# First FFN of a hybrid decoder layer on one Trainium2 core: its RMSNorm from a token-major copy of x, the embedding stores on another queue, and the first 18 steps from a written list

## The chip, the cores and the metric

The kernel runs on 1 core of one Trainium2 chip. The metric is device microseconds of one execution: the median of 3 runs of the kernel before is 1090.26 us (1090.19 to 1090.28). The profile is of one further execution, which took 1090.34 us and whose profiled span is 1088.6 us.

## What is computed

One layer for 512 tokens of width 1024: a SwiGLU FFN, a mixing sub-layer (spatial gating beside a state-space scan), a second FFN, a gated per-layer embedding and a final norm. The change lies in the first FFN and in the embedding's projection, which the kernel computes at its very start.

```python
def rmsnorm(x, g):
    y = x * lax.rsqrt(jnp.mean(x * x, axis=-1, keepdims=True) + EPS)
    return y * g
def swiglu(x, w_gate, w_up, w_down):
    return (jax.nn.silu(x @ w_gate) * (x @ w_up)) @ w_down

h = h + 0.5 * swiglu(rmsnorm(h, ffn1_norm), ffn1_w_gate, ffn1_w_up, ffn1_w_down)
...
h = h + gate * (p @ ple_w_proj)
```

All matrices are float32. Each product is made of three passes of TensorE in a rounded float32 type: high part times high part, high times low, low times high. So every weight and every activation is first split: ScalarE casts the high part (`hi`), VectorE subtracts it from the original (`lo`).

## The kernel before

**Layout.** Activations lie feature-major: `h[0]` to `h[7]` are 128 features by 512 tokens each. FFN weights come in blocks of 128 x 1024 float32 (512 KB): `raw` and `rawb` are the buffers in which they land, `whi`/`wlo` their two parts.

**The FFN in groups of 256 hidden features.** Eleven groups. Group 0 is computed plainly, in four steps (gate and up, upper and lower half of the input features, 128x512 matmuls). Groups 1 to 10 use Strassen's scheme: seven products of 128x256 matmuls (L624) of sums of weight blocks with sums of activation blocks. The sums of activations (`xfa`, `xfb`: the forms x, T1, T2, T3, T4) are made once, by `Early` (L499 to L568): `Early.x` scales h by the norm's gain, `Early.form` adds the blocks (L564, L566), `Early.t` splits the sum (L549, L551), `Early.t1` forms T1 in the buffer `embt` (L535) and lets GpSimd subtract its low part (L539). The sums of weights are made by DMAs of GpSimd's queue that add a second block to one that has landed (L639, L642, L676), and one by VectorE (L634).

**The norm.** The FFN's matmuls run on h times the gain, without the factor 1/rms of a token; that factor comes in behind them, at the gate (L728) and later. `Norm.add` squares h[d] on ScalarE (L247, L250) and adds it up on GpSimd (L251, seven adds); `Norm.sums` lets TensorE add over the features (L261, `ones`, one column for each of 4 token chunks); `of_sums` works out 1/sqrt in 11 small VectorE instructions on 128x4 (L217 to L222); `diagonals` makes two 128x512 tiles of it (L281 to L285); `spread` multiplies them with ones on TensorE (L298), `kept` copies that to SBUF (`rall`, L304).

**Steps and their order.** A `Step` has a load, a split, a product (TensorE) and an `after`. `run` (L347) walks over all steps: product i, split of step i+2, `after` of step i-1, loads six steps ahead. What it records is the order of each engine's queue: TensorE, ScalarE, VectorE and SP run exactly in that order. Steps 0 and 1 are the embedding's two projections, 2 to 5 the plain group, 6 to 14 Strassen group 1 with two down-projection steps in it, and from 15 on group 2. `also` hangs further work on a step (L946 to L959): for instance the squares and T3 on the split of steps 3 and 4, T2 on that of step 6, T1 on 7, T4 on 9.

**The embedding's result** (8 tiles of 128x512, 2 MB) is stored to DRAM by five DMAs of GpSimd's queue (L870), and read back at the kernel's end. Its source tiles are `embt` (two tiles), `p7`, `u2` and two `rawd`, buffers which the FFN uses again later: `embt` for T1.

Of the kernel before, what the change touches and what calls it, by code (L numbers as in the profile page):

```python
# [16 lines left out]

# [20 lines left out]
G_PARTS = (1, 2, 2, 2, 2, 2)  # L38
# [7 lines left out]
LOADS, MIX_LOADS = 6, 4  # L46

# [36 lines left out]
def layer_kernel(ctx: ExitStack, tc: tile.TileContext, a: dict, out: bass.AP):  # L84
# [242 lines left out]

    class Step:


        def __init__(self, product, load=None, sums=None, split=None, after=(), urgent=False):
            self.product, self.load, self.sums, self.split = product, load, sums, split

            self.after, self.urgent = after, urgent
# [11 lines left out]
    def run(steps, opened):  # L346


        n = len(steps)
        held = []  # L350

        def do(i, what):
            if 0 <= i < n and getattr(steps[i], what):
                getattr(steps[i], what)()

        loaded = 0
        for i in range(-3, n + 2):
# [7 lines left out]
            if i in opened:  # L365
                open_region("right", opened[i])
                while held:
                    do(held.pop(0), "load")
            late = 0 <= i - 1 < n and not steps[i - 1].urgent
            do(i + 2, "cast")  # L370
            if 0 <= i - 2 < n and len(steps[i - 2].after) > 1:
                steps[i - 2].after[1]()
            for what in ("split", "after") if late else ("after", "split"):
                if what == "split":
                    do(i + 2, "split")
                    do(i + 3, "sums")
                elif 0 <= i - 1 < n and steps[i - 1].after:
                    steps[i - 1].after[0]()
            do(i - 1, "post")
            do(i, "rest")  # L380

    def also(step, what, fn):

        if what == "after":
            old = step.after[0] if step.after else lambda: None
            step.after = (lambda: (old(), fn()),) + tuple(step.after[1:])
        else:
            old = getattr(step, what) or (lambda: None)
            setattr(step, what, lambda: (old(), fn()))
# [5 lines left out]
    class Parts:  # L395
# [18 lines left out]
        def split(self, raw=None, x=""):  # L414
# [5 lines left out]
            return self.hi, self.lo  # L420

# [81 lines left out]
    class Early:  # L503
# [8 lines left out]
        def x(both, lower):  # L512

            blocks = []
            for e in both:
                hg = e.hg[lower] = sb(("ghi", "glo")[lower], (P, 2, T))
                for k in range(2):
# [3 lines left out]
                    else:  # L521
                        nc.scalar.activation(hg[:, k], h[d], AF.Copy, scale=col(e.name, d))
                blocks.append((hg.rearrange("p k (s t) -> p s k t", s=2), (e.a, e.b)[lower][:, 0:2]))
            for t, to in blocks:
                nc.scalar.copy(to[:, :, 0], t)
            for t, to in blocks:
                nc.vector.tensor_tensor(to[:, :, 1], t, to[:, :, 0].bitcast(F32), ALU.subtract)

        @staticmethod
        def t1(both):  # L530

            f = sb("embt", (P, 2, 2, HT))
            for n, e in enumerate(both):
                x11, x12 = (e.hg[0].rearrange("p k (s t) -> p s k t", s=2)[:, s] for s in range(2))
                nc.vector.tensor_tensor(f[:, n], x11, x12, ALU.subtract)  # L535
            for n, e in enumerate(both):
                nc.scalar.copy(e.a[:, 1, 0], f[:, n])
            for n, e in enumerate(both):
                nc.gpsimd.tensor_tensor(e.a[:, 1, 1], f[:, n], e.a[:, 1, 0].bitcast(F32), ALU.subtract)  # L539

        @staticmethod
        def t(both, i, formed=False):


            if not formed:
                Early.form(both, i)
            blocks = [(e.f[:, (3, 2, 4).index(i) % 2], e.b[:, {3: 2, 2: 3, 4: 4}[i]]) for e in both]
            for f, to in blocks:
                nc.scalar.copy(to[:, 0], f)  # L549
            for f, to in blocks:  # L550
                nc.vector.tensor_tensor(to[:, 1], f, to[:, 0].bitcast(F32), ALU.subtract)  # L551

        @staticmethod
        def form(both, i):
            n = (3, 2, 4).index(i) % 2
            for e in both:
# [8 lines left out]
                else:  # L565
                    nc.vector.scalar_tensor_tensor(  # L566
                        f, x11 if i == 2 else x21, -1.0, other, ALU.mult, ALU.subtract
                    )  # L568

# [25 lines left out]
    class Group:  # L595


        def __init__(self, src, xfs, shared, j):
            self.src, self.xfs, self.shared, self.j = src, xfs, shared, j
            self.last = j == sum(G_PARTS) - 1  # L600
# [28 lines left out]
        def steps(self):  # L629
# [6 lines left out]
            def load7():  # L636
# [11 lines left out]
                (lambda half=half: (self.gate_sum(half), self.gate(half)), lambda half=half: self.times_r(half))  # L648
                for half in range(2)
            ]  # L650
            if self.j == 1:
                gates[1] = (lambda: (self.gate_sum(1), self.gate(1), up()), gates[1][1])
# [15 lines left out]
        def step(self, i, w, raw, to, fresh, loads, sums, after):  # L668
# [3 lines left out]
            def split():  # L672
                parts[0] = w.split(self.s1 if raw else None)
                if i == 6:

# [14 lines left out]
        def plain_steps(self):  # L690


            def step(w, i, which, lower):
                w_parts = {}

                def split():
                    w_parts[0] = w.split()
# [16 lines left out]
                s = Step(product, lambda: self.load((w, i)), None, split, urgent=lower)  # L714
# [9 lines left out]
        def plain_gate(self):  # L724
            self.g = sb("g", (P, 2, 2, HT))
            for m, ps in enumerate(self.ps["gate"]):
                t = self.g[:, :, m]
                nc.vector.tensor_tensor(t, by_half(ps), by_half(self.shared["r"]), ALU.mult)  # L728
                nc.scalar.activation(t, t, AF.Silu)

        def plain_finish(self):
            for m, ps in enumerate(self.ps["up"]):
                t = self.g[:, :, m]
                nc.vector.tensor_tensor(t, t, by_half(self.shared["r"]), ALU.mult)
# [1063 lines left out]
```

## Time and profile before

| what | value |
|---|---|
| median of 3 runs | 1090.26 us |
| the profiled execution | 1090.34 us |
| its span | 1088.6 us |
| TensorE matmuls busy | 1073.7 us (99%) |
| VectorE busy | 783.3 us (72%) |
| ScalarE busy | 515.3 us (47%) |
| GpSimd busy | 154.1 us (14%) |
| DMA | 161.67 MB, mean 149 GB/s |

Times in a timeline are microseconds from the span's start. A row gives start, duration, engine, line, operation, output<-inputs, sizes and count; in brackets stands the idle time of the engine before it and what ended that. TensorE's matmuls overlap in a pipeline: a row's duration is longer than the distance between two starts, so lost time is read from the starts.

### The profile page before, as it was taken

How to read it: one execution, taken by the hardware profiler on the slowest of the kernel's cores; microseconds unless marked ns; L12 is line 12 of the kernel's file. 1: busy time of each engine (PE TensorE's matmuls, PEld its weight loads, DVE VectorE, ACT ScalarE, POOL GpSimd, SP SyncE). 2: the span in 40 equal slices, each digit the busy share in tenths (PEclk: the TensorE clock that was granted, in tenths of full speed). 3: DMA queues.
4: the chain of work that ended last, by engine and by line, in shares of the span. 5: the costliest groups of instructions: out<-in, count | busy, mean ns of one | idle time of the engine just before them, and what ended most of it. 6: DMA issues, size and time to landing. Idle time of an engine off the chain costs nothing.

```text
span 1088.6 us, 16562 instructions
## 1 busy us (share of the span) xinstructions
PE 1073.7 (99%) x6687; PEld 949.8 (87%) x6687; DVE 783.3 (72%) x1078; ACT 515.3 (47%) x711; POOL 154.1 (14%) x139
## 2 busy tenths in 40 slices
PE   9989999999999999999999999999999999999997
PEld 7889999999998788787878888899999999999886
DVE  7797776666667596756897756678766776767766
ACT  6554443444444455474653434354444344344554
POOL 3400000000000300134133000000000000000311
PEclk9999999999999999999999999999999999999998
DMA  9758756675624233444342333567766666643412
GB/s 363 201 141 232 199 152 181 180 193 137 173 60 135 64 93 102 147 129 134 99 131 77 100 94 113 189 144 213 208 163 169 193 183 185 168 123 99 146 46 78
DMA packets 49037, 161.67 MB, mean 149 GB/s; under 512 B 5568, under 2 KB 5824, under 8 KB 48960
## 3 DMA queue, kind: packets, MB, share of 16 engines
q1 hardware_dynamic: 38288, 124.80, 34.2%
q0 software_dynamic: 9232, 33.56, 17.2%
q10 hardware_dynamic: 1440, 2.26, 0.7%
q8 instruction: 52, 0.85, 0.3%
q14 instruction: 25, 0.20, 0.1%
HBM read 156.33 MB, written 4.26 MB: 148 GB/s over the span
## 4 chain that ended last, share of the span: by engine, by line
PE 87%; DVE 7%; ACT 3%; issue 2%; DMA 1%; SPq 0%; POOL 0%; DVEq 0%; ACTq 0%; POOLq 0%
PE mm L624 18%; PE a L624 14%; PE sm L200 10%; PE sm L199 10%; PE sm L201 10%; PE mm L200 4%; PE mm L201 4%; PE mm L199 4%; PE a L199 3%; PE a L201 3%; PE a L200 3%; DVE wlo L428 2%; ACT whi L424 1%; DMA h<-in_x 1%; PE sm L261 1%
## 5 line engine op out<-in xcount | busy, mean ns | idle before, releaser
L424 ACT CAST whi<-raw 128x1024 fp32r<-128x1024 f32 x138 | 144.4, 1046 | 161.0 <-issue 56.8
L428 DVE TENSOR_TENSOR wlo<-raw,whi 128x1024 fp32r<-128x1024 f32 x137 | 172.8, 1261 | 61.9 <-ACT whi L424 60.8
L624 PE MATMUL mm<-xfb,whi 128*128 128x256 f32 x960 | 166.5, 276 | 0.1
L624 PEld LDWEIGHTS mm<-xfb,whi 128*128 128x128 f32 x960 | 145.9, 188 | 1.8 <-ACT a L738 0.2
L624 PE MATMUL mm<-xfb,wlo 128*128 128x256 f32 x480 | 133.1, 277 | 0.4 <-DVE wlo L428 0.3
L201 PE MATMUL sm<-ghi,wlox 128*128 128x512 f32 x296 | 116.3, 393 | 0.0
L200 PE MATMUL sm<-glo,whix 128*128 128x512 f32 x296 | 115.9, 392 | 0.0
L199 PE MATMUL sm<-ghi,whix 128*128 128x512 f32 x296 | 115.2, 389 | 0.0
L624 PE MATMUL a<-xfb,whi 128*128 128x256 f32 x640 | 111.2, 277 | 0.9 <-DVE g L756 0.9
L624 PEld LDWEIGHTS a<-xfb,whi 128*128 128x128 f32 x640 | 97.7, 188 | 3.1 <-issue 1.5
L624 PEld LDWEIGHTS mm<-xfb,wlo 128*128 128x128 f32 x480 | 90.2, 188 | 0.7 <-DVE wlo L428 0.7
L624 PE MATMUL a<-xfb,wlo 128*128 128x256 f32 x320 | 88.7, 277 | 1.1 <-DVE wlo L428 1.1
L428 DVE TENSOR_TENSOR wlox<-rawd,whix 128x1024 fp32r<-128x1024 f32 (+1 forms) x40 | 45.7, 1142 | 58.6 <-ACT whix L424 58.6
L428 DVE TENSOR_TENSOR wlo<-rawb,whi 128x1024 fp32r<-128x1024 f32 x52 | 64.7, 1246 | 25.1 <-ACT whi L424 24.9
L762 ACT ACTIVATE g<-g 128x512 f32<-128x512 f32 x40 | 25.3, 632 | 108.9 <-DVE g L761 108.9
L639 POOL DMA_DIRECT2D raw<-in_ffn_gu x20 | 17.2, 860 | 387.4 <-DVE h L816 122.9
L251 POOL TENSOR_TENSOR ssum<-ssum,tmp 128x512 f32<-128x512 f32 x33 | 50.2, 1522 | 123.7 <-ACT tmp L250 122.8
L816 DVE SCALAR_TENSOR_TENSOR h<-sm,h 128x512 f32<-128x512 f32 x96 | 63.2, 684 | 5.1 <-PE sm L201 4.5
L424 ACT CAST whi<-rawb 128x1024 fp32r<-128x1024 f32 x52 | 54.1, 1043 | 26.7 <-DVE rawb L634 20.0
L201 PEld LDWEIGHTS sm<-ghi,wlox 128*128 128x128 f32 x296 | 55.6, 188 | 11.7
L199 PEld LDWEIGHTS sm<-ghi,whix 128*128 128x128 f32 x296 | 55.7, 188 | 10.8 <-DVE h L816 0.2
L200 PEld LDWEIGHTS sm<-glo,whix 128*128 128x128 f32 x296 | 55.5, 188 | 10.8
(412 smaller groups left out, 2529.7 us busy)
## 6 DMA issues: line engine op xcount, KB each, us to landing
raw<-in_ffn_gu SPq DMA_DIRECT2D x56, 512.0 KB, 5.7
rawd<-in_ffn_down SPq DMA_DIRECT2D x40, 512.0 KB, 4.1
rawb<-in_ffn_gu SPq DMA_DIRECT2D x32, 512.0 KB, 5.1
raw<-in_ffn_gu POOLq DMA_DIRECT2D x30, 512.0 KB, 5.6
raw<-in_w_in SPq DMA_DIRECT2D x29, 512.0 KB, 3.7
s<-in_ffn_gu SPq DMA_DIRECT2D x20, 512.0 KB, 6.7
s<-in_ffn_gu POOLq DMA_DIRECT2D x20, 512.0 KB, 8.5
raw<-in_w_out SPq DMA_DIRECT2D x16, 512.0 KB, 3.6
```

The source lines that it names most:

```text
L199: nc.tensor.matmul(ps, whi, xhi, start=first, stop=False)
L200: nc.tensor.matmul(ps, whi, xlo, start=False, stop=False)
L201: nc.tensor.matmul(ps, wlo, xhi, start=False, stop=last)
L251: self.engines[i].tensor_tensor(self.totals[i], self.totals[i], sq, ALU.add)
L261: nc.tensor.matmul(ps[:, c : c + 1], part[:, c * P : (c + 1) * P], ones[:, 0:1], start=part is t, stop=part is not t or more is None,)
L424: nc.scalar.copy(self.hi[:, : self.n], self.raw[:, : self.n])
L428: nc.vector.tensor_tensor(self.lo[:, :n], self.raw[:, :n], self.hi[:, :n].bitcast(F32), ALU.subtract)
L624: nc.tensor.matmul(o, wt[:, c], xt, start=fresh and p == m == n == 0, stop=last and n == 2, skip_group_check=True,)
L639: nc.gpsimd.dma_start(w21.raw, self.src[0], accum_op=ALU.add)
L762: nc.scalar.activation(t, t, AF.Silu)
L816: nc.vector.scalar_tensor_tensor(h[d], ps[d], 0.5, h[d], ALU.mult, ALU.add)
```

## The change

Four things are changed together.

1. **The norm of the first FFN** is a `RowNorm`. A second copy of x, token-major (`x_rows`, four chunks of 128 tokens by 1024 features), is a further input. Four DMAs of 512 KB bring it into `whix`, `wlox`, `g` and `s1`, buffers that are idle at that time. Four ScalarE instructions square a chunk and give the sum of a row as accumulator output: the 128x4 sums are there without GpSimd's adds and without TensorE's `sums`.
2. **Where it is asked for**: SP issues the four loads behind the last weight load of the plain group and of product 1 and ahead of the other loads of group 1.
3. **The five stores** of the embedding's result go to SP's queue, behind the loads of group 1.
4. **The first 18 steps' order** is written out: `ENTRY` lists pieces of the tasks (`split3:1` is the first piece of the split of step 3), `run` takes them in that order and everything else as before. To that end the helpers became generators that `yield` between instructions. T2, T4 and T1 are hung on the splits of steps 4, 5 and 6.

```diff
+    class RowNorm(Norm):
+        def load(self, *chunks):
+            for c in chunks:
+                self.rows[c] = sb(self.tags[c], (P, D))
+                nc.sync.dma_start(self.rows[c], self.src[c])
+        def add(self, *chunks):
+            if 0 in chunks:
+                self.squares = sb("rtok", (P, NC))
+            for c in chunks:
+                t = self.rows[c]
+                nc.scalar.activation(t, t, AF.Square, accum_out=self.squares[:, c : c + 1])
+                yield
...
+        for entry in order.split():
+            name, _, count = entry.partition(":")
+            for _ in islice(tasks[name], int(count) if count else None):
+                pass
+        for task in tasks.values():
+            for _ in task:
+                pass
...
     def store_embedding():
         for to, t in stores:
-            nc.gpsimd.dma_start(to, t)
+            nc.sync.dma_start(to, t)
...
-        norm.behind(steps[at:], D, lambda r: (shared.update(r=r), groups[0].plain_gate()))
+        norm.behind([steps[i] for i in (2, 2, 3)] if at else steps, D, gates)
...
-    ffn1_norm = Norm()
+    ffn1_norm = RowNorm(a["x_rows"], "whix", "wlox", "g", "s1")
...
-    also(steps[3], "split", lambda: (squares(0, 1), Early.x(early, 1), squares(2, 3)))
-    also(steps[4], "split", lambda: (Early.t(early, 3), squares(4, 5, 6, 7), store_embedding()))
-    also(steps[6], "split", lambda: Early.t(early, 2))
...
+    also(steps[6], "load", lambda: ffn1_norm.load(0, 1, 2, 3))
+    also(steps[3], "split", lambda: Early.x(early, 1))
+    also(steps[9], "load", store_embedding)
+    also(steps[4], "split", lambda: Early.t(early, 3))
+    also(steps[4], "split", lambda: Early.t(early, 2))
+    also(steps[5], "split", lambda: ffn1_norm.add(0, 1, 2))
+    also(steps[6], "split", lambda: ffn1_norm.add(3))
+    also(steps[5], "split", lambda: Early.form(early, 4))
+    also(steps[6], "split", lambda: Early.t1(early))
+    also(steps[5], "split", lambda: Early.t(early, 4, True))
```

**SP's queue, from the loads of group 1 on.** `rawb_150` is the last weight of the plain group, `rawb_178` that of product 1, the rest is for the products behind it. Before:

```order
L408 DMA rawb_150<-in_ffn_gu 128x1024
L408 DMA rawb_178<-in_ffn_gu 128x1024
L408 DMA raw_212<-in_ffn_gu 128x1024
L641 DMA s_59_215<-in_ffn_gu 128x1024
L408 DMA raw_218<-in_ffn_gu 128x1024
L408 DMA rawb_280<-in_ffn_gu 128x1024
L408 DMA rawd_475<-in_ffn_down 128x512
```

Now:

```order
L475 DMA rawb_178<-in_ffn_gu 128x1024
L354 DMA whix_180<-in_x_rows 128x1024
L354 DMA wlox_182<-in_x_rows 128x1024
L354 DMA g_184<-in_x_rows 128x1024
L354 DMA s_55_186<-in_x_rows 128x1024
L475 DMA raw_226<-in_ffn_gu 128x1024
L726 DMA s_65_229<-in_ffn_gu 128x1024
L475 DMA raw_232<-in_ffn_gu 128x1024
L475 DMA rawb_285<-in_ffn_gu 128x1024
L967 DMA emb_dram<-embt_262 128x1024
L967 DMA emb_dram<-p_72_265 128x512
```

The four row loads stand ahead of four weight loads, and the stores, which were not on this queue, behind them.

**VectorE's queue, around the norm's small instructions.** The place is the one between the plain group's last two products. Before, behind the diagonals (the rows end with the gate of the plain group):

```order
L285 TENSOR_TENSOR tmp_457<-ident_72,tokp_452 128x512
L428 TENSOR_TENSOR wlo_462<-raw_212,whi_461 128x1024
L566 SCALAR_TENSOR_TENSOR ghi_318<-glo_264,ghi_318 128x512
L566 SCALAR_TENSOR_TENSOR glo_320<-glo_267,glo_320 128x512
L535 TENSOR_TENSOR embt_468<-ghi_168 128x512
L535 TENSOR_TENSOR embt_468<-ghi_171 128x512
L728 TENSOR_TENSOR g_505<-sm_282,rall_503 128x2x256
```

Now, the rows ahead of the norm's first small instructions (`nv`, `ny`):

```order
L650 SCALAR_TENSOR_TENSOR glo_275<-glo_223,glo_275 128x512
L614 TENSOR_TENSOR embt_370<-ghi_167 128x512
L634 TENSOR_TENSOR xfb_110<-ghi_272,xfb_110 128x512
L634 TENSOR_TENSOR xfb_112<-glo_275,xfb_112 128x512
L504 TENSOR_TENSOR wlo_401<-rawb_178,whi_400 128x1024
L614 TENSOR_TENSOR embt_370<-ghi_171 128x512
L233 TENSOR_SCALAR nv_435<-rtok_323 128x4
L234 TENSOR_SCALAR ny_436<-nv_435 128x4
```

T4's and T1's work stood behind the norm's small instructions and now stands ahead of them; the first write of `embt_370` has to wait until the store of `embt_262`, the same memory, has landed.

**GpSimd's queue.** Before:

```order
L251 TENSOR_TENSOR ssum_259<-ssum_259,tmp_277 128x512
L870 DMA emb_dram<-rawd_308 128x1024
L639 DMA raw_212<-in_ffn_gu 128x1024
L642 DMA s_59_215<-in_ffn_gu 128x1024
L251 TENSOR_TENSOR ssum_259<-ssum_259,tmp_326 128x512
L870 DMA emb_dram<-rawd_311 128x1024
L251 TENSOR_TENSOR ssum_259<-ssum_259,tmp_329 128x512
```

Now, the whole of it up to group 2:

```order
L724 DMA raw_226<-in_ffn_gu 128x1024
L727 DMA s_65_229<-in_ffn_gu 128x1024
L620 TENSOR_TENSOR xfa_109<-embt_370,xfa_109 128x512
L620 TENSOR_TENSOR xfa_111<-embt_370,xfa_111 128x512
L724 DMA raw_609<-in_ffn_gu 128x1024
```

Adds and stores are gone from it; the two accumulating loads and T1's two subtractions, which both were there before, follow each other. On TensorE the only difference is that the eight one-column matmuls of `sums` (L261) are gone.

## Prediction before the run

> **What bounds the kernel now.** First the busy times of the page, then TensorE's own timeline, then windows of it.
>
> ```profile
> PE 1073.7 (99%) x6687; PEld 949.8 (87%) x6687; DVE 783.3 (72%) x1078; ACT 515.3 (47%) x711; POOL 154.1 (14%) x139
> ```
>
> TensorE is busy 99% of the span, and the change takes from it eight one-column matmuls. So it can pay only where TensorE stands still or runs slowly in the first 18 steps, up to about 80 us. The distance between two starts shows these places: elsewhere it is 0.23 us for a 128x512 matmul (34.69 to 34.92 below) and 0.11 for a 128x256 one (53.98 to 54.09).
>
> ```profile
> 34.69 0.39 PE L200 MATMUL sm<-xfb,whi 128*128 128x512 f32 x1
> 34.92 0.40 PE L201 MATMUL sm<-xfb,wlo 128*128 128x512 f32 x1
> 36.41 1.05 PE L261 MATMUL sm<-ones,ssum 128*128 128x1 f32 x8 [1.09 <-POOL ssum L251]
> 37.33 0.48 PE L199 MATMUL mm<-xfb,whi 128*128 128x512 f32 x1
> ...
> 50.36 0.28 PE L624 MATMUL mm<-xfb,wlo 128*128 128x256 f32 x1
> 51.47 0.39 PE L624 MATMUL mm<-xfb,wlo 128*128 128x256 f32 x1 [0.28 <-DVE wlo L428]
> ...
> 53.98 0.28 PE L624 MATMUL mm<-xfb,wlo 128*128 128x256 f32 x1
> 54.09 0.47 PE L624 MATMUL a<-xfb,whi 128*128 128x256 f32 x2
> 55.31 0.38 PE L624 MATMUL a<-xfb,wlo 128*128 128x256 f32 x1 [0.75 <-DVE wlo L428]
> ...
> 60.71 0.28 PE L624 MATMUL mm<-xfb,wlo 128*128 128x256 f32 x1
> 62.00 0.50 PE L624 MATMUL a<-xfa,whi 128*128 128x256 f32 x2 [1.00 <-ACT u L746]
> 62.34 0.28 PE L624 MATMUL a<-xfa,wlo 128*128 128x256 f32 x1
> ...
> 67.50 0.40 PE L201 MATMUL sm<-ghi,wlo 128*128 128x512 f32 x1
> 68.80 0.48 PE L624 MATMUL a<-xfb,whi 128*128 128x256 f32 x2 [0.91 <-DVE g L756]
> ```
>
> The next view is TensorE's windows; the columns are length, busy time with count of PE, PEld, DVE, ACT and POOL, the granted clock, DMA share and GB/s.
>
> ```profile
> 35.18:38.59 3.41, 2.32 (x15) 1.95 (x15) 3.33 (x5) 1.65 (x3) 1.18 (x1) 1.00 0.34 126
> 38.59:42.01 3.42, 3.42 (x10) 2.66 (x9) 3.01 (x16) 2.00 (x3) 0.00 (x0) 0.50 0.84 251
> 59.07:62.49 3.42, 2.42 (x21) 2.21 (x20) 3.39 (x4) 2.08 (x4) 0.00 (x0) 1.00 0.39 77
> ```
>
> Three losses can be read:
> - **The sums.** From 34.92 to 37.33 are 2.41 us where one matmul takes 0.23: 2.18 lost, waiting for GpSimd's adds and in the eight one-column matmuls.
> - **The half clock.** The 3.42 us behind it ran at a granted clock of 0.50: 1.71 lost.
> - **Four waits for split operands**: 50.36 to 51.47 (1.11, of which three matmuls take 0.34: 0.77), 54.09 to 55.31 (1.22 less 0.23: 0.99), 60.71 to 62.00 (1.29 less 0.11: 1.18), 67.50 to 68.80 (1.30 less 0.23: 1.07). Together 4.01, and 0.11 at each restart (62.00 to 62.34 is 0.34 where two take 0.23), 0.44 in all: 4.45.
>
> The sum is 8.3 us. That is all there is to win, 0.8%.
>
> **The change part by part.**
>
> *The norm's sums.* Removed: eight squares on ScalarE, seven adds on GpSimd, eight matmuls. Added: four squares of 128x1024 with an accumulator.
>
> ```profile
> 30.07 0.63 ACT L250 ACTIVATE tmp<-h 128x512 f32<-128x512 f32 x1 [0.43 <-POOL ssum L251]
> 40.42 0.20 ACT L951 ACTIVATE warm<-ones 128x1 f32<-128x1 f32 x1
> ...
> L424 ACT CAST whi<-raw 128x1024 fp32r<-128x1024 f32 x138 | 144.4, 1046 | 161.0 <-issue 56.8
> ```
>
> Eight times 0.63 is 5.0 us. No row shows an accumulator output; a square of 128x1024 lies between the cast's 1.05 and, if the sum comes out by an instruction of its own, 1.05 + 0.20: 4.2 to 5.0 for four. I take 5.0, no difference; ScalarE's order puts the last square ahead of T1's casts, so it is done before VectorE reaches the norm. It costs nothing on TensorE. The 2.18 us of the first loss go.
>
> *VectorE without GpSimd beside it.*
>
> ```profile
> 24.16 2.05 DVE L428 TENSOR_TENSOR wlo<-raw,whi 128x1024 fp32r<-128x1024 f32 x1 [0.34 <-ACT whi L424]
> 31.67 3.57 DVE L428 TENSOR_TENSOR wlo<-rawb,whi 128x1024 fp32r<-128x1024 f32 x2 [2.88 <-ACT whi L424]
> 35.16 1.75 DVE L566 SCALAR_TENSOR_TENSOR ghi<-ghi,ghi 128x512 f32<-128x512 f32 x1
> 38.20 0.68 DVE L551 TENSOR_TENSOR xfb<-glo,xfb 128x512 fp32r<-128x512 f32 x1
> 42.45 1.22 DVE L428 TENSOR_TENSOR wlo<-raw,whi 128x1024 fp32r<-128x1024 f32 x1
> ...
> 30.61 5.75 POOL L251 TENSOR_TENSOR ssum<-ssum,tmp 128x512 f32<-128x512 f32 x3
> 46.83 2.87 POOL L539 TENSOR_TENSOR xfa<-embt,xfa 128x512 fp32r<-128x512 f32 x2
> ```
>
> Beside GpSimd's adds these rows take 2.05, 3.57 and 1.75 instead of 1.22, 2.44 and 0.68: 3.0 us that VectorE gets back. With them, and with T2 and T4 formed in its idle time before 31.67 (2.88 us), the weight splits of products 7 to 5 no longer stand behind T4's and T1's forming. I put the four waits at zero: the norm's diagonals are followed by those splits at once, 1.22 us each, while product 1 alone keeps TensorE 48 x 0.113 = 5.4 us. If that cover is gone they cost what they cost now, up to 4.45.
>
> *The new wait.* The first half of T1 (L614) writes `embt`, and must wait until `embt`'s store has landed; it stands on VectorE ahead of the norm. Behind it are queued T4's low parts, the split of product 1's weights, T1's second half, the norm's 13 small instructions and the two diagonals, and TensorE's spread matmul, between the plain group and product 1, waits for the last. So: when does the store land?
>
> ```profile
> 15.72 0.43 SPq L408 DMA_DIRECT2D rawb<-in_ffn_gu  x1
> rawb<-in_ffn_gu SPq DMA_DIRECT2D x1, 512.0 KB, 11.9
> 19.00:24.00 5.00, 5.00 (x23) 3.99 (x23) 4.09 (x6) 4.82 (x7) 2.36 (x3) 1.00 1.01 412
> raw<-in_ffn_gu POOLq DMA_DIRECT2D x1, 512.0 KB, 5.8
> s<-in_ffn_gu POOLq DMA_DIRECT2D x1, 512.0 KB, 7.3
> rawd<-in_ffn_down SPq DMA_DIRECT2D x1, 256.0 KB, 6.9
> rawd<-in_ffn_down SPq DMA_DIRECT2D x4, 256.0 KB, 4.1
> ```
>
> The last weight load of this burst lands 11.9 us after 15.72, at 27.6. At 412 GB/s, stores and loads together (19 to 24 us), a 512 KB DMA takes 1.3 us; four row loads ahead of it add 5.1, and the stores of 1.05 MB (`embt`, `p7`, `u2`) that now share the engines with it are gone from its side, which takes off 2.6: 30.1. The `embt` store comes next: alone it lands at 31.4. But GpSimd's accumulating load of `raw` goes out when that weight has landed, three places earlier (26.2). Two such, issued at 44.99 and 46.26, land 5.8 and 7.3 us later (the rows are of these), at 50.8 and 53.6: 2.8 us each, so its data starts some 3 us behind its issue, at 29.2. If the two alternate evenly, both are done 1.3 + 2.8 = 4.1 us after 30.1: 34.2. I take 33.0, near the middle of 31.4 and 34.2. The stores behind it hold up little: next on SP stand the down loads, which waited for the stores of their `rawd` buffers before, too. An end farther off is the down load's row: beside accumulating loads 256 KB took 6.9 instead of 4.1, 2.8 more; for 512 KB 5.6 more, 37.0.
>
> From the landing on, VectorE needs:
>
> ```profile
> 38.80 0.15 DVE L217 TENSOR_SCALAR nv<-sm 128x4 f32<-128x4 f32 x1
> 41.25 1.29 DVE L285 TENSOR_TENSOR tmp<-ident,tokp 128x512 fp32r<-128x512 f32 x2
> 44.79 1.29 DVE L535 TENSOR_TENSOR embt<-ghi 128x512 f32<-128x512 f32 x2
> ...
> 527.68 1.31 POOL L1358 TENSOR_TENSOR xs<-xs,tmp 128x512 f32<-128x512 f32 x1
> 527.86 1.15 DVE L221 SCALAR_TENSOR_TENSOR nt<-nt,nv 128x4 f32<-128x4 f32 x1
> ```
>
> T1's halves 1.29, two low parts 1.2, a split 1.2, the small instructions 2.45 (38.80 to 41.25), the diagonals 1.29: 7.4 us, so 40.4. T1's two subtractions on GpSimd, which today run beside VectorE's reads of PSUM, now fall into this chain. A small instruction of another norm took 1.15 beside one such GpSimd instruction (0.15 at 38.80): 1.0 lost to each, 1.1 as these take 1.43 instead of 1.31, 2.2 for both: 42.6. Below this is zero, if they fall elsewhere. TensorE comes to the spread 25 matmuls behind 34.92, at 40.75: a wait of 1.9, with the restart 2.0. Bounds: 31.4 + 7.4 = 38.8, no wait; 34.2 + 9.6 = 43.8, 3.0.
>
> *The half clock.* Behind the sums it cost 1.71. The new wait is about as long as the old gap, but begins 1.3 us before 42.01, where a window of the old spacing ends, and is cut in two; the window 59.07:62.49 lost 1.0 and the clock stayed at 1.00. I take full clock, and the other as a rival. The Trainium skill, page "TensorE: Matmul & The Clock Gate" (part 1, "What's actually happening"), says that the clock falls to half after an idle window of about 3.4 us. By that rule neither gap would halve it. The trace differs: in 35.18:38.59 TensorE was busy for 2.32 us, and the next window had 0.50.
>
> *Sum.* 8.3 won, 2.0 paid: 6.3. Against the profiled execution's 1090.34 that is 1084.0; its own time lies 0.08 over the median, so for the median too.
>
> **The rivals.**
> - *Half clock behind the new wait.* For it: the old gap of 2.2 us had it. Against: the cut at 42.01. 1084.0 + 1.7 = 1085.7.
> - *No wait.* The store lands at 31.4, or GpSimd's subtractions miss the small instructions. For it: with a landing at 31.4 the chain ends at 41.0 even with both subtractions, 0.25 late. 1090.3 - 8.3 = 1082.0.
> - *The list does not do what it says*: the four waits stay, since VectorE comes out of the norm later than TensorE wants. Then only 2.18 + 1.71 are won and 2.0 paid: 1088.5. Against: 5.4 us of product 1 as cover.
> - *Slower: the store starves.* Place: VectorE's wait before T1. Each us of landing past 33.0 is a us of TensorE. At 37.0 the wait is 6.0; so long an idle time would bring the half clock for up to two windows, 3.4: 6.0 + 3.4 - 8.3 = 1.1 lost, 1091.4. It decides from a landing at 35.9 with the half clock (4.9 + 3.4), at 39.3 without. For it: the 6.9 us of the down load. Against: a landing later than 34.2 needs less than an even share, and beside plain stores the engines kept 412 GB/s.
>
> **How the numbers follow.** Forecast 0.45, half clock 0.20, no wait 0.16, waits stay 0.11, slower 0.08. The forecast's own range is 1082.8 to 1085.0 (waits of 3.0 to 0.8). The range 1081.8 to 1087.0 holds the first three and leaves out the last two. A measurement of this kernel can tell about 0.2% (2.2 us) from no change: faster is below 1088.1, so forecast, half clock, no wait and a little of the fourth: 0.83; slower is above 1092.4, the starved store's worse half: 0.04; the rest 0.13.
>
> **What would show it.** Right: no L261 matmuls before 100 us; a wait of about 2 us of the spread matmul for VectorE's `tmp` near 41 to 43; VectorE's `embt` instruction waiting for a DMA until about 33; a small norm instruction of over 1 us beside GpSimd; no bracket of 0.3 us or more on TensorE from 45 to 80. Wrong: the clock at 0.50 in a window near 45; `embt`'s store landing past 36; new waits for `wlo` or for row chunks (then the loads ahead of the weights cost more than I gave them, zero).

## The result and the profile after

| kernel | executions | us | ratio to before |
|---|---|---|---|
| before | 4 | 1090.27 median (1090.19 to 1091.44) | |
| after, first | 4 | 1084.26 median (1082.95, 1083.06, 1085.46, 1086.01) | 0.9943 (0.9924 to 0.9963) |
| after, again | 5 | 1085.72 median (1083.34, 1083.59, 1085.72, 1086.11, 1086.15) | 0.9953 (0.9939 to 0.9967) |
| after, third | 5 | 1083.81 median (1082.52, 1082.54, 1083.81, 1085.08, 1085.65) | 0.9937 (0.9924 to 0.9949) |

The forecast was 1084.0. The 14 executions lie in two groups, seven from 1082.5 to 1083.8 with a mean granted clock of 0.997 or 0.998, seven from 1085.1 to 1086.2 with 0.996 or 0.997 (three of the 14, in both groups, have 0.997, so the mean clock alone does not part them). The forecast lies between the groups, and what parts them is the main question below.

The first line of the page of after (1082.95 us, of the lower group): TensorE does 4.4 us less than before, GpSimd 14.7 us less.

```profile
PE 1069.3 (99%) x6679; PEld 946.3 (88%) x6679; DVE 780.3 (72%) x1078; ACT 515.6 (48%) x711; POOL 139.4 (13%) x127
```

TensorE's timeline where the norm's factor is spread. The one-column matmuls of L261 are gone, and between 44 and 112 us no two matmuls stand further apart than their spacing by more than 0.15 us: all four waits for split operands are gone.

```profile
40.34 0.40 PE L217 MATMUL a<-xfb,wlo 128*128 128x512 f32 x1
41.81 1.10 PE L314 MATMUL sm<-tmp,onesr 128*128 128x512 f32 x2 [1.07 <-DVE tmp L301]
42.75 0.40 PE L709 MATMUL mm<-xfa,whi 128*128 128x256 f32 x2
```

From 40.34 to 41.81 are 1.47, one matmul takes 0.23: a wait of 1.24. From 41.81 to 42.75 are 0.94 instead of the 0.47 of two matmuls: the second diagonal is waited for too. Together 1.7.

VectorE's timeline in front of it, then GpSimd's two T1 subtractions of the same profile.

```profile
32.91 0.69 DVE L614 TENSOR_TENSOR embt<-ghi 128x512 f32<-128x512 f32 x1 [1.49 <-DMA emb_dram<-embt]
34.73 2.33 DVE L504 TENSOR_TENSOR wlo<-rawb,whi 128x1024 fp32r<-128x1024 f32 x1
38.57 1.20 DVE L236 TENSOR_TENSOR nt<-ny 128x4 f32<-128x4 f32 x1
41.07 1.29 DVE L301 TENSOR_TENSOR tmp<-ident,tokp 128x512 fp32r<-128x512 f32 x2
```

```profile
34.68 1.30 POOL L620 TENSOR_TENSOR xfa<-embt,xfa 128x512 fp32r<-128x512 f32 x1 [6.01 <-ACT xfa L617]
38.45 1.30 POOL L620 TENSOR_TENSOR xfa<-embt,xfa 128x512 fp32r<-128x512 f32 x1 [2.47 <-ACT xfa L617]
```

VectorE stood still for 1.49 until the store of `embt` had landed. Then a weight split took 2.33 instead of 1.22 and one small norm instruction 1.20 instead of 0.16, each beside one of GpSimd's subtractions. The diagonals are done at 42.36.

The theory taken into the experiments (A): the wait of TensorE at the spread needs both the late landing of the store and what GpSimd takes from VectorE. Its rivals were that one of them alone makes it, or that the written list's order does. For the two groups of times: half clock behind this wait (H), later with a late landing as what brings it (W), against some other cause (S).

### The profile page after: what moved, and what is told of

Same layout as the page of the kernel before. It is cut to its first block, busy times and chain, and to the rows that moved or that the text cites. A ratio compares the mean times of both kernels' runs of the same rounds, so it can differ in the third digit from the quotient of the medians.

```text
span 1081.2 us, 16536 instructions
## 1 busy us (share of the span) xinstructions
PE 1069.3 (99%) x6679; PEld 946.3 (88%) x6679; DVE 780.3 (72%) x1078; ACT 515.6 (48%) x711; POOL 139.4 (13%) x127
## 4 chain that ended last, share of the span: by engine, by line
PE 88%; DVE 6%; DMA 3%; ACT 2%; issue 1%; DVEq 0%; SPq 0%; ACTq 0%
PE mm L709 20%; PE a L709 15%; PE sm L216 10%; PE sm L215 10%; PE sm L217 10%; PE mm L216 4%; PE mm L215 4%; PE mm L217 4%; PE a L215 3%; PE a L217 3%; PE a L216 3%; DMA emb_dram<-embt 1%; DVE wlo L504 1%; DMA whix<-in_x_rows 1%; DMA raw<-in_ffn_gu 1%
## 5 line engine op out<-in xcount | busy, mean ns | idle before, releaser
L217 PEld LDWEIGHTS sm<-ghi,wlox 128*128 128x128 f32 x296 | 55.5, 188 | 11.7
L216 PEld LDWEIGHTS sm<-glo,whix 128*128 128x128 f32 x296 | 55.5, 188 | 10.8
L709 PEld LDWEIGHTS a<-xfb,wlo 128*128 128x128 f32 x320 | 60.1, 188 | 0.6 <-DVE wlo L504 0.6
```

Source lines behind the costliest of these rows:

```text
L216: nc.tensor.matmul(ps, whi, xlo, start=False, stop=False)
L217: nc.tensor.matmul(ps, wlo, xhi, start=False, stop=last)
L709: nc.tensor.matmul(o, wt[:, c], xt, start=fresh and p == m == n == 0, stop=last and n == 2, skip_group_check=True,)
```

## The experiments

**T1 in another buffer.** Nothing waits for the store.

```diff
-            f = sb("embt", (P, 2, 2, HT))
+            f = sb("whix", (P, 2, 2, HT))
```

> T1 is formed in the tile of the first row chunk (`whix`), whose last reader is a square on ScalarE before 30 us, instead of in `embt`, whose store lands at 32.9. Theory A (the store's landing begins the chain that ends at the spread): VectorE's L614 starts at about 31.4 instead of 32.91, the diagonals are done 1.2 to 1.5 us sooner, TensorE's spread wait falls from 1.24 to 0.3 or less, and the time from 1083.0 to 1081.6 (1081.3 to 1082.2), without executions near 1085.5 to 1086. Rival B (the chain is bounded by GpSimd's two subtractions and by ScalarE's T1 casts, not by the landing): the spread starts within 0.3 us of 41.81 as before and the time stays at 1083.0, with some executions near 1086.

1081.53 us median (1081.21 to 1082.16, 4 executions; ratio 0.9918, 0.9905 to 0.9932). VectorE's and TensorE's timelines:

```profile
31.43 0.69 DVE L614 TENSOR_TENSOR whix<-ghi 128x512 f32<-128x512 f32 x1
34.97 1.28 DVE L233 TENSOR_SCALAR nv<-rtok 128x4 f32<-128x4 f32 x1
36.28 1.22 DVE L234 TENSOR_SCALAR ny<-nv 128x4 int32<-128x4 int32 x1
39.60 1.29 DVE L301 TENSOR_TENSOR tmp<-ident,tokp 128x512 fp32r<-128x512 f32 x2
```

```profile
40.43 0.40 PE L217 MATMUL a<-xfb,wlo 128*128 128x512 f32 x1
40.67 0.77 PE L314 MATMUL sm<-tmp,onesr 128*128 128x512 f32 x2
41.27 0.40 PE L709 MATMUL mm<-xfa,whi 128*128 128x256 f32 x2
```

T1 starts at 31.43 and the spread waits for nothing, although both subtractions still hit the norm's small instructions (1.28 and 1.22). The store landed at 33.68 in this very execution, later than in the first profile of after, and it did no harm. As A has it; B falls. (One accumulating load of GpSimd also moved two places ahead, since GpSimd's order is not fixed.)

**T1 behind the norm.** Only the list is changed.

```diff
-load9 product3 split5.1 split5.2 split6.2:1 split5.3 product4 split6 split6.1 split6.2:1
-split6.2 product5 after4 after4.1 split7 split7.1 load12 product6 split8 after5 product7 sums9
+load9 product3 split5.1 split5.2 split5.3 product4 split6 split6.1
+product5 after4 after4.1 split7 split7.1 load12 product6 split8 after5 split6.2 product7 sums9
```

> Only the written list is changed: all six pieces of T1 stand behind the norm (after `after5`), since product 5 is the first to read T1. Theory A: the norm's small instructions and diagonals no longer stand behind the store's landing or beside GpSimd's two subtractions; the diagonals are done near 38 to 39, the spread matmul does not wait, 1.2 + 0.5 us are won: 1081.3 (1080.8 to 1081.9), and no execution near 1086. Rival B: VectorE's two T1 instructions (1.3 us) now stand ahead of the splits of product 7 or 2 and GpSimd's two fall beside those, so one of the old waits of 0.8 to 1.0 us comes back: 1082.0 to 1082.5.

1082.51 us (1082.14 to 1082.77, 5 executions). The spread starts at 40.65 without a wait, and a wait comes back at the fourth product behind it:

```profile
49.49 0.40 PE L709 MATMUL a<-xfb,whi 128*128 128x256 f32 x2
50.50 0.38 PE L709 MATMUL a<-xfb,wlo 128*128 128x256 f32 x1 [0.62 <-DVE wlo L504]
```

Both theories had a part: A on the spread, B on the price, 0.8 at one place. VectorE's work has to stand somewhere, and behind the norm it has no slack either. No execution came above 1083.

**T1's low parts on VectorE.** The store is waited for, GpSimd's subtractions are taken out.

```diff
-                nc.gpsimd.tensor_tensor(e.a[:, 1, 1], f[:, n], e.a[:, 1, 0].bitcast(F32), ALU.subtract)
+                nc.vector.tensor_tensor(e.a[:, 1, 1], f[:, n], e.a[:, 1, 0].bitcast(F32), ALU.subtract)
...
-split6.2 product5 after4 after4.1 split7 split7.1 load12 product6 split8 after5 product7 sums9
+split6.2:2 product5 after4 after4.1 split7 split7.1 load12 product6 split8 after5 split6.2 product7 sums9
```

> T1's two low parts are subtracted on VectorE, behind the norm and the gate, instead of on GpSimd; T1 itself still waits for the store of `embt`. Theory A (two causes are needed for the wait at the spread: the store's landing at 32.9 and 1.1 us that each of GpSimd's two subtractions takes from VectorE): the split L504 that took 2.33 takes 1.2, the small norm instruction that took 1.20 takes 0.16, the diagonals are done 2.1 us sooner, near 40.3, and the spread does not wait (L314 at 40.6 to 40.9). VectorE's two extra instructions of 0.7 us behind the gate bring back a wait of up to 0.9 near 49.6, as the run with T1 behind the norm showed: 1081.4 to 1082.5, with no execution above 1085. Rival B (the landing alone makes the wait, VectorE has slack elsewhere): the spread still waits 1.0 us or more and the time is 1083.0 or above.

1083.7 us (1082.62 to 1084.27, 4 executions). VectorE's timeline:

```profile
34.47 0.69 DVE L614 TENSOR_TENSOR embt<-ghi 128x512 f32<-128x512 f32 x1 [2.82 <-DMA emb_dram<-embt]
36.28 1.22 DVE L504 TENSOR_TENSOR wlo<-rawb,whi 128x1024 fp32r<-128x1024 f32 x1
40.48 1.29 DVE L301 TENSOR_TENSOR tmp<-ident,tokp 128x512 fp32r<-128x512 f32 x2
```

From T1 to the end of the diagonals are 7.30 us, against 9.45 in after (32.91 to 42.36): GpSimd's two subtractions cost the chain 2.15. But the store landed 1.6 later than in the first profile of after, though nothing ahead of it was changed, so the spread still waited 0.42. From a landing at 32.9 the same 7.30 would end at 40.2, ahead of TensorE, which comes at 40.57. So A is right for this landing only: from about 33.3 on (40.57 less 7.30) the landing alone makes a wait. The time lies above the expectation since two waits came back near 62 us (idle for 0.37 and 0.75, 1.5 lost together) where one near 49.6 was expected.

**The gap of after filled.**

```diff
-                got["ps"] = self.spread(got["diags"])
+                ps = sm_ps()
+                for _ in range(5):
+                    nc.tensor.matmul(by_half(ps), ones_r, x_ffn1[0].a[:, 0:2, 0], start=True, stop=True)
+                got["ps"] = self.spread(got["diags"], ps)
```

> Five extra matmuls of 128x512 (1.15 us) on data that is long there stand ahead of the spread matmul and fill most of TensorE's wait; they write the bank that the spread then overwrites, so nothing that the kernel computes changes. Theory H (the executions at 1085.5 to 1086 are those in which TensorE's clock falls to half behind the idle time at the spread): all executions lie within 0.5 us of 1083.0, with a mean granted clock of 0.998. Rival S (the slower executions have another cause, such as the clock at the start or the transfers): executions near 1085.5 to 1086 remain, about half of them, with 0.996 to 0.997.

1083.4 us (1082.58, 1083.39, 1083.40, 1084.17, 1085.90). Three of five lie within H's 0.5 of 1083.0; 1084.17 lies 1.2 above it, at a mean clock of 0.999, and 1085.90 with the upper group, at 0.996. The profiled one had its store landed early, at 32.5, and shows no half clock. Inconclusive: five fillers cover 1.2 us, and a later landing, as in the experiment above, would leave a gap behind them.

**A longer wait.**

```diff
+                extra = tmp()
+                for _ in range(2):
+                    nc.vector.tensor_tensor(extra, h[0], h[0], ALU.mult)
                 tok = self.of_sums(self.squares, n)
```

> The changed kernel with two extra VectorE multiplications of 128x512 (0.68 us each) ahead of the norm's small instructions, whose result nothing uses: the wait at the spread grows by 1.36, to about 2.6. Theory H (idle time at the spread brings half clock, the more surely the longer it is): 0.50 in the window behind it in most executions, 1.36 + 1.7 over the changed kernel's faster group: 1086.3 (1085.9 to 1087), and the group at 1083 to 1084.6 is gone or rare. Rival S (the slower group has another cause): two groups as before, moved by 1.36: 1084.5 and 1087.2.

1084.44 us (1084.08, 1084.28, 1084.60, 1088.11). The profile shows why this decided little: the store landed early, at 32.15, so the wait was 1.23, no longer than in after, and the clock behind it 1.00. The execution at 1088.11 had a mean clock of 0.994, 0.004 under the first. One window of 3.41 at 0.50 takes 0.0016 off the mean of 1084 us, so by this estimate it had two or three of them. It was not profiled.

**After, again and a third time.**

> The changed kernel without an edit, beside the others. Theory H (half clock behind the spread's wait in some executions): two groups again, 1082.9 to 1083.2 with a mean clock of 0.998 and 1085.4 to 1086.1 with 0.996 to 0.997; if the profiled one is of the slower group, its windows show 0.50 in the window that begins behind 40.6. Rival S: the groups are not told apart by the clock, or the profiled one of the slower group loses its time elsewhere.

> The changed kernel again, on the chip of the other three, for one more look at when the `embt` store lands and at the spread of its times. Theory W: two groups, 1082.9 to 1083.6 with a mean clock of 0.998 and 1085.4 to 1086.2 with 0.996 to 0.997; in a profile of the faster group the store lands by 33.0 and the clock behind the spread is 1.00, in one of the slower group it lands after 33.5 and the clock is 0.50.

Two groups both times. The second profile was of the lower group (T1 at 32.70, spread at 41.57, clock 1.00). The third was of the upper one, 1085.65. Its VectorE and TensorE timelines:

```profile
33.80 0.69 DVE L614 TENSOR_TENSOR embt<-ghi 128x512 f32<-128x512 f32 x1 [2.21 <-DMA emb_dram<-embt]
41.92 1.29 DVE L301 TENSOR_TENSOR tmp<-ident,tokp 128x512 fp32r<-128x512 f32 x2
```

```profile
40.52 0.40 PE L217 MATMUL a<-xfb,wlo 128*128 128x512 f32 x1
42.66 1.19 PE L314 MATMUL sm<-tmp,onesr 128*128 128x512 f32 x2 [1.74 <-DVE tmp L301]
43.65 0.63 PE L709 MATMUL mm<-xfa,whi 128*128 128x256 f32 x2
```

TensorE's windows of the third profile, then of the first (columns as in the prediction: the second number is TensorE's busy time, the one ahead of the DMA share the granted clock):

```profile
40.11:43.52 3.41, 1.56 (x6) 0.77 (x5) 3.17 (x11) 2.49 (x4) 0.49 (x1) 1.00 0.48 150
43.52:46.93 3.41, 3.41 (x17) 3.32 (x17) 3.41 (x5) 1.40 (x3) 0.00 (x0) 0.50 0.85 276
```

```profile
40.15:43.57 3.42, 2.24 (x13) 1.46 (x12) 3.25 (x10) 2.20 (x4) 0.00 (x0) 1.00 0.61 175
43.57:46.98 3.41, 3.41 (x33) 3.41 (x32) 3.41 (x5) 1.72 (x3) 0.00 (x0) 1.00 0.97 361
```

The store landed 0.9 later, the spread 0.85 later, and the window behind ran at 0.50: in it 17 matmuls instead of 33, and the 144 matmuls from the spread on took 1.6 longer. 0.85 + 1.6 is 2.5 of the 2.7 us between the two executions. W holds for this pair. That all seven upper executions are of this kind was not shown; their mean clocks, 0.996 or 0.997, allow it.

One step ahead the landing itself has two kinds. In the eight profiles with this order of transfers the store landed at 33.68 to 34.45 in the three in which the plain weight `s` ahead of it landed at 28.9 or 29.0, and at 32.15 to 33.54 in the five in which that weight landed at 27.4 to 28.0. What moves `s` stays open.

**The gap of before filled.** Five extra matmuls ahead of the eight one-column ones.

```diff
             def sums():
-                got["ps"] = self.sums()
+                ps = sm_ps()
+                for _ in range(5 if self is ffn1_norm else 0):
+                    nc.tensor.matmul(by_half(ps), ones_r, x_ffn1[0].a[:, 0:2, 0], start=True, stop=True)
+                got["ps"] = self.sums(ps=ps)
```

> The kernel before, with five extra matmuls of 128x512 ahead of the norm's eight one-column matmuls, which fill the 1.1 us in which TensorE waited for GpSimd's last add; nothing that is computed changes. Theory H (the window at half clock behind the sums is brought by the idle time there, and costs 1.7 us): the window of 0.50 near 38.6 to 42.0 is gone and the time falls by 1.7, to 1088.6 (1088.3 to 1089.2). Rival S (the half clock has another cause, or its time is hidden because the split operands that TensorE waits for later set its end): 1090.0 to 1090.5 as before.

1091.16 us (11 executions) against 1090.7 of before: ratio 1.0003 (0.9995 to 1.0012). The half clock is gone (39.37 to 42.79 at 1.00, 16 matmuls instead of 10), the spread starts at 43.03 instead of 44.56, and nothing is won:

```profile
50.72 0.50 PE L627 MATMUL mm<-xfb,whi 128*128 128x256 f32 x2 [1.63 <-ACT a L741]
51.50 0.39 PE L627 MATMUL mm<-xfb,wlo 128*128 128x256 f32 x1 [0.28 <-DVE wlo L431]
```

The row at 51.50 is the one at 51.47 in the kernel before. TensorE came 1.5 us sooner and waited 1.63 for ScalarE's copy `a<-mm`, behind which the bank can be written again; then, as in the kernel before, it waited for VectorE's split `wlo`, which sets 51.5. ScalarE's timeline of before and VectorE's row of that split, which this kernel repeats within 0.1 us:

```profile
45.51 1.23 ACT L537 CAST xfa<-embt 128x512 fp32r<-128x512 f32 x2 [4.89 <-DVE embt L535]
46.64 0.58 ACT L304 COPY rall<-sm 128x512 f32<-128x512 f32 x1
47.98 1.23 ACT L729 ACTIVATE g<-g 128x512 f32<-128x512 f32 x2 [0.76 <-DVE g L728]
49.12 1.04 ACT L424 CAST whi<-rawb 128x1024 fp32r<-128x1024 f32 x1
50.06 0.58 ACT L738 COPY a<-mm 128x512 f32<-128x512 f32 x1
50.19 1.23 DVE L428 TENSOR_TENSOR wlo<-rawb,whi 128x1024 fp32r<-128x1024 f32 x1 [1.64 <-ACT whi L424]
```

The chain ran from VectorE's late T1 over its casts, the spread factor's copy and the gate to the cast `whi` and its split, done at 51.42; the copy stands behind the same gate. TensorE's clock was not on it. H is right that the idle time brings the half clock, S about its price: of the 1.7 us only 0.28 got past 51.5 (a matmul at 55.03 instead of 55.31). In this profile a wait for `wlox` at 106.12, which the profile of before does not have, lost 1.1 again.

**The stores on GpSimd's queue**, in the list at before's place.

```diff
-            nc.sync.dma_start(to, t)
+            nc.gpsimd.dma_start(to, t)
...
-after1:1 after1 split4 split5.1:1 split4.2:2 split5:1 split4.2:2 split5 split5.1:1 split4.2
-load9 product3 split5.1 split5.2 split6.2:1 split5.3 product4 split6 split6.1 split6.2:1
+after1:1 after1 split4 load9 split5.1:1 split4.2:2 split5:1 split4.2:2 split5 split5.1:1 split4.2
+product3 split5.1 split5.2 split6.2:1 split5.3 product4 split6 split6.1 split6.2:1
```

> The stores of the embedding go out on GpSimd's queue at the place of before (behind the forming of T3), ahead of the accumulating loads, instead of on SP's queue behind the weights; all else as in the changed kernel. Theory A (the wait at the spread begins with the store's landing): the `embt` store lands before 30 us, T1 does not wait, the spread waits 0.3 at most, and the time is 1081.6 (1081.3 to 1082.3) if the weights and row chunks, which then share the engines with 2.5 MB of stores, are still in time. Rival B (loads that come later cost as much as the wait: the last row chunk lands at 27 or later instead of 24.8, the Strassen weights at 33 instead of 30.8, and ScalarE's squares and casts, in their written order, are late): 1083 to 1086 with new waits of TensorE for `wlo` before 60 us.

1082.23 us (1081.85 to 1083.04, 4 executions; ratio 0.9921, 0.9906 to 0.9936). The `embt` store went out at 17.47 and landed at 24.64, the spread (41.09) did not wait. The last row chunk landed at 27.5, the last Strassen weight at 37.3 instead of 30.8, and TensorE stood still for neither. The time lies in A's range. The stores' new place behind the weights, by itself, loses time.

**The store later.**

```diff
-        for to, t in stores:
+        for to, t in stores[1:3] + stores[:1] + stores[3:]:
```

> The changed kernel, with the store of `embt` asked for behind those of `p` and `u` (512 KB) instead of ahead of them, so that it lands 1.3 to 2.1 us later. Theory W (the executions at 1085.5 to 1086 are those in which the `embt` store lands late and half clock follows on the longer wait): L614 starts at 34.2 to 35.0 instead of 32.9, the wait at the spread is 1.3 to 2.1 longer, the clock falls to 0.50 behind it in most executions: 1086.0 to 1087.0, seldom below 1085. Rival L (late landings alone, no half clock): 1084.5 to 1085.3 with a clock of 1.00 behind the wait. Rival S (neither): 1083 and 1086 in two groups as before.

1089.97 us (1088.37 to 1091.45, 11 executions; ratio 0.9994, 0.9985 to 1.0003): the whole gain is gone. The store landed not 1.3 to 2.1 but 6.3 us later, at 39.2. VectorE's, TensorE's and the windows' rows:

```profile
39.21 0.69 DVE L614 TENSOR_TENSOR embt<-ghi 128x512 f32<-128x512 f32 x1 [7.64 <-DMA emb_dram<-embt]
```

```profile
48.02 1.40 PE L314 MATMUL sm<-tmp,onesr 128*128 128x512 f32 x2 [7.12 <-DVE tmp L301]
```

```profile
42.74:46.15 3.41, 0.00 (x0) 0.00 (x0) 3.20 (x9) 2.13 (x3) 1.27 (x1) 1.00 0.84 270
46.15:49.57 3.42, 1.55 (x4) 1.14 (x5) 3.21 (x10) 1.97 (x4) 0.86 (x1) 0.50 0.68 273
49.57:52.98 3.41, 3.41 (x18) 3.41 (x17) 3.41 (x5) 1.70 (x3) 0.86 (x1) 0.50 0.88 149
```

W's direction, with a size that no theory had: 512 KB of stores ahead of it cost 6.3 us of landing. GpSimd's accumulating loads were under way by then (from 32 to 35 us 101 packets of them beside 110 of SP's); that they are the cause is argued from this and the next run.

**The rows behind the Strassen weights.** Only the list is changed.

```diff
-load6 load6.1 product0 split2 split3.1:3 split3.1:1 load7 product1 after0 split3:1 split4.1:1
-split3 split4.1:1 split3.1:1 split4.1:2 split3.1:1 split4.1:1 split3.1 split4.1 load8 product2
+load6 product0 split2 split3.1:3 split3.1:1 load7 product1 after0 split3:1 split4.1:1
+split3 split4.1:1 split3.1:1 split4.1:2 split3.1:1 split4.1:1 split3.1 split4.1 load8 load6.1 product2
```

> Only the written list is changed: the four row chunks are asked for behind the Strassen weights (and still ahead of the stores) instead of ahead of them. Theory A (the rows' place ahead of the weights wins nothing; only the store's landing and GpSimd's two subtractions set the spread): the Strassen weights land 5 us sooner, the rows 5 us later (the last near 31), ScalarE's squares still end before 36, the `embt` store lands within 0.7 of 32.9, and the time is that of the changed kernel, 1082.9 to 1083.6 in its faster group. Rival B (ScalarE takes its instructions in the written order, so the first square, waiting for its rows until 27, holds the casts of the weights behind it): waits of TensorE for `wlo` or `whi` before 40 us, 1084 to 1087.

1089.49 us (1089.04 to 1090.42, 10 executions; ratio 0.9987, 0.9978 to 0.9996). Both theories fall. ScalarE held up a split by 0.65 only, but the store landed at 37.13:

```profile
37.15 0.69 DVE L614 TENSOR_TENSOR embt<-ghi 128x512 f32<-128x512 f32 x1 [4.87 <-DMA emb_dram<-embt]
```

The DMA view of the issues between 13 and 22 us: out and in, queue, size, median us from issue to landing.

```profile
whix<-in_x_rows SPq DMA_DIRECT2D x1, 512.0 KB, 10.1
wlox<-in_x_rows SPq DMA_DIRECT2D x1, 512.0 KB, 11.9
g<-in_x_rows SPq DMA_DIRECT2D x1, 512.0 KB, 14.5
s<-in_x_rows SPq DMA_DIRECT2D x1, 512.0 KB, 15.8
```

Issued 1.1 to 1.3 us apart, the four land at 26.5, 29.5, 33.4 and 35.9: 2.5 to 3.9 us each, where the same chunks ahead of the weights landed 1.28 apart (21.00, 22.28, 23.56, 24.83 in after). GpSimd's accumulating load goes out when the weight under it has landed. With the weights first that is 22.0 instead of 26.8, and all that SP has still to move shares the engines with it.

The Trainium skill, page "DMA: Bandwidth & Descriptors" (section "Queues, rings and completion order"), says that each DMA engine goes round the queues that have work for it, a packet at a time. The trace agrees: from 28 to 32 us GpSimd's queue (q0) and SP's (q1) moved nearly the same number of packets (columns: packets, MB, share of the time of the 16 engines).

```profile
q0 software_dynamic: 153, 0.56, 70.3%
q1 hardware_dynamic: 150, 0.55, 36.9%
```

But the engines spent about 0.29 us on a packet of the accumulating loads and 0.16 on a plain one; with SP's queue alone (after, 15 to 25 us, 1128 packets at 103.0%) a plain one took 0.15. So an even share of the packets left the plain side about a third of the engines' time. Turn by turn, 512 KB would take 1.28 x 0.45 / 0.15, an estimate of 3.8 us, near the longest of the four.

**The planner's own order.** The list is emptied; the norm from the rows, the loads and the stores stay.

```diff
 ENTRY = """
-load0 load1 load1.1 load2 load3 load3.1 load4 load5 split0 split1:1 split1.1:2 split1 split1.1
...
-split17
 """
```

> The written list is empty: the pieces run in the planner's own order, while the row loads, the norm from them, the stores on SP's queue and the assignment of T2, T3, T4 and T1 to steps stay as changed. Theory A (the gain is mostly from the norm's adds leaving GpSimd and from T4 and T2 formed before the norm, which the steps already do): within 1.5 us of the changed kernel's faster group, 1083 to 1084.5, with a wait of 1 to 2.5 at the spread and no waits for `wlo` behind it. Rival B (the list carries the gain of the four waits): waits of 0.7 to 1.2 for `wlo` come back at three or four places between 45 and 70 us: 1086 to 1088.

1087.63 us (1086.99 to 1088.66, 8 executions; ratio 0.9969, 0.9958 to 0.9979). Besides the spread's wait of 1.5 there is one other:

```profile
65.70 0.68 PE L709 MATMUL a<-xfb,whi 128*128 128x256 f32 x2 [2.58 <-DVE g L845]
```

```profile
62.37:65.78 3.41, 0.83 (x5) 0.38 (x4) 2.62 (x5) 1.14 (x2) 0.00 (x0) 1.00 0.00 0
65.78:69.20 3.42, 3.42 (x17) 3.42 (x18) 3.08 (x5) 1.57 (x2) 0.00 (x0) 0.50 0.86 230
```

VectorE reads the bank `a` (L845) only behind a gate that waits for ScalarE. A wait of 2.7 and half clock behind it, 1.7: in this execution, 4.4 together, this is what the list saves. B's size, but in one wait at one place instead of three or four.

## Why the prediction came out, point by point

- **What there was to win.** Predicted 8.3, so 1082.0 without a new wait. The kernel without one (T1 in another buffer) took 1081.53, 8.9 under before in the same comparison. Near it as a sum.
- **Its parts.** Wrong: the half clock was counted as 1.71 won by itself. Taken away alone it wins nothing (ratio 1.0003), since a chain over VectorE and ScalarE set the end of the stretch at 51.5 either way. The change also took GpSimd's adds and T1's late forming out of that chain; that the 8.3 came in full because of this is argued from the rows, not tested. Losses on TensorE's timeline were added as if each could be had alone.
- **The squares at no cost.** Right. Four squares of 1.05 with a read of the accumulator of 0.2 behind each (rows below); as the rows overlap, ScalarE was busy with them for 4.5 us, within the estimate's 4.2 to 5.0, and the last was done at 34.1.
- **The four waits at zero.** Right for the list as written. Without it one wait of 2.7 with half clock comes, and with T1 moved behind the norm one of 0.8. The cover was wrong: product 1 is 24 matmuls, not 48, and lasts 2.7 us (42.75 to 45.48), not 5.4; the splits stood far enough ahead all the same.
- **The landing at 33.0.** 32.89 in the first profile. In the eight profiles with this order of transfers (three of after, and the runs that changed T1, the gap or the wait) it lay from 32.15 to 34.45: between the bounds of 31.4 and 34.2 but once, 0.25 above the upper one. The share of GpSimd's accumulating loads was the right thing to look for.
- **The chain of 7.4 and 2.2 for GpSimd.** 7.30 without the subtractions, 9.45 with them: 2.15.
- **The wait of 2.0.** 1.7 in the first profile; TensorE came at 40.57 instead of 40.75, and the chain ended at 42.36 instead of 42.6. In the third, 2.4.
- **Full clock behind it.** The step that failed. It was taken with 0.45 against 0.20; half of the executions lie where the rival put them (1085.7), and the one that was profiled had the window at 0.50. The argument by the place of the windows of one profile could not hold: whether a window loses enough depends on where it happens to lie and on a landing that moves by 2 us. The row 35.18:38.59, by which the prediction argued, is a weak measure too: of its 2.32 us busy, 1.05 were the eight one-column matmuls. The Trainium skill's rule that it was weighed against ("TensorE: Matmul & The Clock Gate", part 1) asks for an idle window; the third profile's window was busy for 1.56 of 3.41 and the next had 0.50, so the trace differs again.
- **Slower, the store starves.** The mechanism is real: with the landing at 37.1 or 39.2 two windows ran at 0.50. The size was too high, 1091.4 at 37.0 against 1090.42 in the profiled execution, with the landing at 37.13 (the median of ten is 1089.49). The first of the two windows began 0.8 before TensorE had work again, which is 0.4 of it; the rest was not traced.
- **The sum.** Against the profiled 1090.34 the first profile won 7.4, not 6.3 and not 8.3 - 1.7 = 6.6. Of the other 0.8, 0.18 were won before 40 us, and about 0.3 by a closer spacing of matmuls (below); the rest was not traced. 1084.0 lies between the two groups of executions; that it is near the median is luck, since the groups balance.

What three parts of the change are worth, each undone alone, against 1084.45, the median of the 14: the rows ahead of the weights 5.0 us, the list 3.2, the stores behind the weights a loss of 2.2. Against the lower group alone (median 1083.06) these are 6.4, 4.6 and 0.8. The runs are of several chips, on which the kernel before differed by 0.5. The norm from rows itself was not undone alone. T1 in another buffer keeps the stores where they are and takes away the wait: it beats both kernels, 1081.53.

## What to carry to other kernels

A loss on the busiest engine's timeline is worth what the next wait leaves of it: before adding such losses up, ask of each which engine sets the end of its stretch. Where an instruction writes a buffer that a store is still reading, its landing is a time that moved here by 2 us from one execution to the next; give it another buffer or put the store ahead, and profile several executions, not one. And count which transfers start an accumulating load: 512 KB that moved beside one took two to three times as long here.

## What was not expected

- **The clock falls on a window that is partly busy.** After windows at full clock, next windows at 0.50 followed on 1.56 and 0.83 us busy of 3.41, at 1.00 on 2.24, 2.25 and (before, gap filled) 2.03. In the run with the later store 1.58 was followed by a window at 1.00, in which no matmul ran. So for such windows the border lay somewhere from 1.56 to 2.03, but for one: before, 2.32 was followed by 0.50, and there 1.05 were the one-column matmuls, which would have to count for little. After a window that itself ran at 0.50, even 2.60 (rows behind the weights) was followed by 0.50. What exactly is counted stays open.
- **Matmuls of 128x256 have two spacings.** Nine take 1.02 us in the first profile of after and 1.06 in the second (start to start), with the clock at 1.00 in both:

```profile
43.10 0.39 PE L709 MATMUL mm<-xfa,whi 128*128 128x256 f32 x2
44.12 0.39 PE L709 MATMUL mm<-xfa,whi 128*128 128x256 f32 x2
```

  In the second they start at 43.21 and 44.27. The difference lasts until the next 128x512 matmuls, 144 matmuls and 0.65 us. The kernel before has the wider one for some 66 matmuls between 55.5 and 64.8 us, where the first profile of after has the closer one: the 0.3 us above. What chooses between them stays open.
- **The accumulator's read is an instruction of its own**, here in ScalarE's timeline of after:

```profile
24.28 1.07 ACT L361 ACTIVATE whix<-whix 128x1024 f32<-128x1024 f32 x1
25.24 0.20 ACT L361 ACTIVATION_READ_ACCUMULATOR whix<-whix 128x1 f32 x1
```
